# Projections beside the attention: steps of six products in place of twelve

## The chip, the cores and the metric

One core of a Trainium2 chip runs the whole kernel. The metric is the device time in microseconds (us), lower is better; the median of several runs stands for a kernel.

## The reference, cut to what matters

One layer of a decoder trunk on 1,024 tokens of width 1,024, with 16 learned meta tokens put ahead (1,040 positions). Everything is float32.

```python
h = h + 0.5 * swiglu(rms_norm(h, ffn1_norm), ffn1_w_in, ffn1_w_out)
u = rms_norm(h, mix_norm) @ w_in                 # 1024 -> 3584 columns
hq, hf, hi, hg, sq, sk, sv = split(u)            # 7 x 512 columns
o_hg = hgrn2(hq, hf, hi, hg, ...)                # gated linear recurrence, 4 heads of 128
o_sb = stick_breaking(sq, sk, sv, ...)           # causal attention, 8 heads of 64
h = h + concat(o_hg, o_sb) @ w_out
h = h + 0.5 * swiglu(rms_norm(h, ffn2_norm), ffn2_w_in, ffn2_w_out)
```

hgrn2 works in chunks of 128 positions; stick_breaking takes blocks of 128 queries: sigmoids of the scores, a running product of (1 - sigmoid) towards older keys, and the weighted sum of the values.

## The kernel before, in words

The kernel runs in stages, one after the other on TensorE (PE): the first feed-forward block; the projection `u`; attention; the recurrence; the output projection; the second feed-forward block. PE's order is written by hand (`manual_schedule`): PE executes in the order in which the Python code emits. The other engines are ordered by the framework.

**Products.** A matrix product of float32 quality is made of three products of rounded parts: each operand is split into a high and a low half (`wh`, `wl`; `xh`, `xl`), and for every k tile of 128 rows there are `wh*xh` (L249), `wl*xh` (L250) and `wh*xl` (L251). A projection column (128 columns of `w_in`) has 8 k tiles, so 24 products for each piece of positions. They add up in one PSUM bank.

**The projections of the recurrence** (`hgrn_fill`, L1118). There are 16 columns, in the order v, f, q, g for each of heads 0 to 3. A column of kind v or f is made in four pieces (264 or 256 positions), one of kind q or g in two halves of 512. The generator hands out a list of steps, each with a planned cost in ns; a step before is half of the k tiles of a piece, twelve products. After the last step of a piece, `use` (L1127) reads the bank out: a copy for v (L1135), two sigmoids for f (L1141, L1142), a sigmoid and then a VectorE product that reads the bank once more for q and g (L1149, L1150). The first step of a column issues the load of the next column's weights.

These steps are dealt out in three places.

1. *Projection stage* (`tasks`, L2153): the first two columns, through a planner called `weave`, beside preparation of the attention's operands, which has no PE instruction.
2. *The braid* (L1694): most of the other steps, beside the attention. Attention comes as 32 jobs (8 heads of 4 pairs of query blocks), one a round. A job's scores (tile `z`, L1640 and L1641) run in its own round, the transposes of its weights (`flip`, L1495 and L1549) two rounds later, the products with the values (`oacc`, L1570 and L1572) three rounds later. The transposes use two PSUM buffers, each freed when ScalarE (L1618) and VectorE (L1619) have split it into `wu` or `wm`. Scores go through two buffers, freed by two sigmoids (L1642, L1643), and then a scan on VectorE (L1646). All the projections of this stretch share one PSUM bank, since the other holds a constant (`begin`). In each round, projection steps are taken while a debt is positive, and are spread evenly over it:

```python
owed += share * sum(t for _, t, _ in now)   # share is 1.22
while owed > 0:
    step = next(fill, None)
    ...
    owed -= step[0]
now += [(at + (i + 0.5) / len(more), t, f) for i, (t, f) in enumerate(more)]
```

3. *The rest* (`rest`, L2201): what the braid has not taken and the last column (g of head 3), through `weave` (L1724) beside the recurrence heads 0, 1 and 2. The weave keeps a clock of planned PE time. A projection step adds its cost. A stage of a head adds its PE cost and then holds that head for a lag. The heads may start at 9000, 14000 and 19000. The choice here:

```python
ready = bool(live) and live[0][0] <= clock
if filling and join is None and (behind or not ready and (even or not live)):
    step = next(fill, None)
```

In this call `even` is always true and `behind` never, and the weave ends with the last projection step; stages that heads have not yet done are carried on by the next weave (L2267). That one mixes heads 0 to 3 with the 64 steps of three products of the first half of the output projection (tile `wo`, `mix_out`, 16 column tiles of four steps; weights in two buffers, attention's output in tiles `oT`), and there `behind` and `even` keep the steps spent in proportion to the heads' planned work.

**A recurrence head** (`hgrn_attend`, L1185) has these stages (planned PE cost, lag, in ns): loads (0, 4000); flips of v (960, 500); "own", 16 small matmuls (1740, 1700; L1235, then VectorE L1236 and L1239); seven levels for n = 1 to 64 (890, 1500 each; a copy on ScalarE L1264, eight matmuls L1270, two decays on VectorE L1257, and for n up to 16 a predicated copy on VectorE L1278, otherwise copies on ScalarE L1288); flips of k (960, 2000; L1299, L1306); states (1740, 2500; L1314, L1321, VectorE L1324); two outputs (1740, 3000; L1334, L1338); two closing flips (430, 0; L1354).

Of the kernel before, what the change touches and what calls it, by code (L numbers as in the profile page):

```python
# [22 lines left out]
KT = D // P  # L23
# [25 lines left out]
class Block:  # L49
# [1068 lines left out]
    def hgrn_fill(self, xh, xl, pool, dst):  # L1118

        nc = self.nc  # L1120
        plan, cols = self.heads_plan, self.columns_of_heads()
        self.stores, self.level_banks = [], "zo"

        def staged(n):
            return pool.tile([P, 512], F32, tag="st", name="st", bufs=4)[:, :n]

        def use(kind, h, ps, c0, n):  # L1127
            s = slice(c0, c0 + n) if kind in "vf" else slice(c0 - META, c0 - META + n)
            t = staged(n)
            if c0 >= HALVES[1][0] and kind != "g":  # L1130
                ps = ps[:, ::-1]
                at = s.start + HALVES[1][0] + T - 2 * c0 - n
                s = slice(at, at + n)
            if kind == "v":
                nc.scalar.copy(t, ps)  # L1135
                with self.tc.issue_after(self.last_load.ins):
                    nc.sync.dma_start(dst[kind][h, :, s], t)
                return
            elif kind == "f":
                k = staged(n)  # L1140
                nc.scalar.activation(t, ps, AF.Sigmoid)  # L1141
                nc.scalar.activation(k, ps, AF.Sigmoid, scale=-1.0)  # L1142
                nc.vector.tensor_scalar(
                    t, t, self.lbc[:, h : h + 1], self.lb[:, h : h + 1], ALU.mult, ALU.add
                )
                nc.vector.tensor_scalar_mul(k, k, self.lbc[:, h : h + 1])
                nc.sync.dma_start(dst["k"][h, :, s], k)
            else:
                nc.scalar.activation(t, ps, AF.Sigmoid)  # L1149
                nc.vector.tensor_mul(t, t, ps)  # L1150
            store = lambda: nc.sync.dma_start(dst[kind][h, :, s], t)
            if (kind, h) == plan[-1] and c0 == HALVES[1][0]:
                self.stores.append(store)
            else:
                store()

        kept = {}

        def part(i, ci, c0, n, half):
            if ci == 0 and half == 0:  # L1160
                kept["w"] = self.ahead_w.pop(cols[i])
                for c in cols[i + 1 : i + (3 if i == 0 else 2)]:
                    if c not in self.ahead_w:
                        self.ahead_w[c] = self.col_tile(self.a["w_in"][0], c)
                kept["round"] = self.rounds[cols[1]]
            if half == 0:
                kept["ps"] = self.proj_bank(n)
            self.product(
                kept["ps"], kept["w"], xh, xl, c0, n, range(4 * half, 4 * half + 4)
            )  # L1170
            if half == 1:
                with self.tc.issue_after(kept["round"]) if i == 0 else ExitStack():
                    use(*plan[i], kept["ps"], c0, n)

        for i, (kind, _) in enumerate(plan):
            for ci, (c0, n) in enumerate(PIECES if kind in "vf" else HALVES):
                for half in range(2):
                    yield 12 * (n * 0.42 + 13), lambda a=(i, ci, c0, n, half): part(*a)

    def level_bank(self, shape, name):  # L1180
        self.level_banks = self.level_banks[::-1]
# [592 lines left out]
    def run(self):  # L1774
        nc, tc, a = self.nc, self.tc, self.a
# [11 lines left out]
        n = 512  # L1787
# [8 lines left out]
        with ExitStack() as c0:  # L1796
            with ExitStack() as c1:
# [117 lines left out]
                with tc.manual_schedule(engines={nc.tensor.engine}), ExitStack() as c2:  # L1915
# [181 lines left out]
                    xh, xl = hat  # L2097
# [52 lines left out]
                columns = self.hgrn_fill(xh, xl, pst, hgD)  # L2150
                oH, self.att = [], []

                def tasks():  # L2153
                    done = []
                    for i in range(4):
                        for x in done[i - 2] if i > 1 else ():
                            yield "join", x
                        done.append(
                            (yield from self.sb_project(i, xh, xl, mixb, mix, (qD, kD, vD)))
                        )  # L2160
                        if i == 2:
                            next(jobs)
                    for t, f in islice(columns, 16):
                        f()
                        yield t

                with tc.manual_schedule(engines={nc.tensor.engine}):
                    cf = ExitStack()
                    fetch = self.pool("fetch", ctx=cf, side="right")
                    jobs = self.sb_jobs((qD, kD, vD, oD), fetch, self.att)  # L2170
                    with ExitStack() as c2:
                        mixb = self.pool("mixb", ctx=c2)
                        mix = self.pool("mix", ctx=c2)
                        self.weave(tasks())
                    with ExitStack() as c2:
                        self.att.append(self.pool("att1", ctx=c2))
                        tag = self.proj_tags[0]
                        self.proj_tags = [self.proj_tags[1]] * 2
                        self.begin = self.pproj.tile([P, 512], F32, tag=tag, name="begin", bufs=1)
                        nc.vector.memset(self.begin, 0.0)  # L2180
                        nc.vector.tensor_copy(self.begin[:, 1 : P + 1], self.ident[:, ::-1])
                        self.braid(jobs, islice(columns, 76), 1.22, 2.0, 3.0)
                    cf.close()
                    self.proj_tags[0] = tag
                    hg_ctx = ExitStack()
                    hg = self.pool("hg", ctx=hg_ctx, side="right")
                    heads = [self.hgrn_attend(h, hg, hgD, oH) for h in range(4)]
                    self.wide = hg.tile([P, 5, 512], U8, name="wide")
                    for i, n in enumerate(LEVELS[:5]):
                        m = self.masks[:, i, :].rearrange("p (b h r) -> p b h r", h=2, r=n)  # L2190
                        wide = self.wide[:, i].rearrange("p (h c x) -> p h c x", h=2, c=4)
                        for half in range(2):
                            for c in range(4):
                                nc.vector.tensor_copy(
                                    wide[:, half, c].rearrange("p (b r) -> p b r", r=n),
                                    m[:, :, 1 - half, :],
                                )
                    for h in range(3):
                        next(heads[h])

                    def rest():  # L2201
                        left = list(columns)
                        for t, f in left[:-1]:
                            f()
                            yield t
                        left[-1][1]()

                    self.weave(rest(), heads[:3], 1e6, 1.0, True)
# [183 lines left out]
```

## Time and profile before

| what | value |
|---|---|
| median of the runs | 1957.84 us (1956.85 to 1957.93, 3 runs) |
| profiled execution, its own time | 1959.65 us |
| span from first to last instruction | 1957.9 us |
| granted PE clock, mean | 0.999 |
| busy in the span: PE, VectorE (DVE), ScalarE (ACT), GpSimd (POOL) | 98%, 71%, 43%, 23% |

In the profile an instruction is named by its line in the kernel (L1270), its engine and the tiles it writes and reads (`out<-in`). PEld are the weight loads of PE. A row of a group gives count, busy us, mean ns of one instruction, the idle time of the engine before them and what ended it. A row of the waits says who waited for whom: us in total, times, longest. A matmul's shown length (0.39 us for 512 columns) overlaps the next; from start to start it is 0.23 us. SPq is the queue that issues most DMAs.

### The profile page before, as it was taken

The numbers are of one execution on the slowest core, as the hardware profiler recorded it, in microseconds if no ns is written. First come the engines' busy times: TensorE is split into PE (matmuls) and PEld (weight loads), VectorE is DVE, ScalarE is ACT, GpSimd is POOL, SyncE is SP. The second block draws the span as 40 slices with busy tenths as digits, with TensorE's granted clock in tenths as the row PEclk, the third lists the DMA queues.
The fourth block names the chain that finished last, engine by engine and source line by source line (L and its number), as shares of the span: only waits on it lengthen the run. The fifth ranks groups of instructions, "written<-read, shape, count | busy, mean of one in ns | idle before, by whom it ended". The sixth has DMA issues, their size and how long they took to land.

```text
span 1957.9 us, 30218 instructions
## 1 busy us (share of the span) xinstructions
PE 1919.8 (98%) x10607; PEld 1616.6 (83%) x10607; DVE 1390.4 (71%) x2184; ACT 849.6 (43%) x1711; POOL 450.5 (23%) x625
## 2 busy tenths in 40 slices
PE   7999999999999999999999999999999999999999
PEld 6888888788888888888898978887888888888887
DVE  7977877877678665467777766677567767766774
ACT  6523443334444544356666635433232332344443
POOL 3010100001000003133333332210544645530000
PEclk9999999999999999999999999999999999999999
DMA  7356887758965315865454177655634444469473
GB/s 213 93 165 170 253 272 243 233 203 291 375 221 188 127 54 144 193 170 148 128 148 121 57 253 225 161 208 183 198 115 140 128 131 121 132 243 318 154 231 113
DMA packets 381687, 355.54 MB, mean 182 GB/s; under 512 B 129040, under 2 KB 284560, under 8 KB 381536
## 3 DMA queue, kind: packets, MB, share of 16 engines
q1 hardware_dynamic: 359728, 288.98, 48.7%
q0 software_dynamic: 20768, 64.63, 9.5%
q8 instruction: 84, 1.38, 0.3%
q14 instruction: 67, 0.55, 0.1%
q10 hardware_dynamic: 1040, 0.00, 0.0%
HBM read 237.95 MB, written 115.57 MB: 181 GB/s over the span
## 4 chain that ended last, share of the span: by engine, by line
PE 89%; DVE 4%; DMA 3%; ACT 2%; issue 1%; POOL 1%; SPq 1%; DVEq 0%; ACTq 0%; POOLq 0%
PE o L732 21%; PE qb L450 18%; PE qa L450 12%; PE qc L450 12%; PE proj L249 5%; PE proj L251 4%; PE proj L250 4%; PE flip L1495 2%; PE wo L250 1%; PE wo L249 1%; PE wo L251 1%; PE mq L1001 1%; PE oacc L1572 1%; PE oacc L1570 1%; DMA oT<-oD 1%
## 5 line engine op out<-in xcount | busy, mean ns | idle before, releaser
L450 PE MATMUL qb<-T,wh 128*128 128x512 f32 x1056 | 344.6, 390 | 1.3 <-ACT T L309 0.8
L450 PEld LDWEIGHTS qb<-T,wh 128*128 128x128 f32 x1056 | 198.1, 188 | 46.4 <-issue 2.5
L450 PE MATMUL qa<-B,wh 128*128 128x512 f32 x696 | 226.7, 390 | 0.3 <-ACT B L835 0.2
L249 PE MATMUL proj<-xh,wh 128*128 128x512 f32 (+2 forms) x640 | 213.2, 333 | 2.6 <-ACT st L1142 1.3
L732 PE MATMUL o<-t,w 128*128 128x512 f32 x924 | 211.8, 390 | 0.7 <-DVE u L543 0.7
L251 PE MATMUL proj<-xl,wh 128*128 128x512 f32 (+2 forms) x640 | 210.2, 328 | 0.8 <-DVE xl L1957 0.8
L250 PE MATMUL proj<-xh,wl 128*128 128x512 f32 (+2 forms) x640 | 210.1, 328 | 0.0
L732 PE MATMUL o<-parts 128*128 128x512 f32 x924 | 209.6, 389 | 0.0
L450 PE MATMUL qb<-T,wl 128*128 128x512 f32 x528 | 205.5, 389 | 0.0
L732 PEld LDWEIGHTS o<-t,w 128*128 128x128 f32 x924 | 172.8, 188 | 37.8 <-ACT sgm L981 1.1
L732 PEld LDWEIGHTS o<-parts 128*128 128x128 f32 x924 | 173.5, 188 | 36.0
L362 DVE TENSOR_TENSOR wl<-s,wh 128x512 fp32r<-128x512 f32 x160 | 165.6, 1035 | 50.8 <-ACT wh L360 49.9
L360 ACT CAST wh<-s 128x512 fp32r<-128x512 f32 x160 | 99.2, 622 | 188.5 <-PE qb L450 141.1
L450 PEld LDWEIGHTS qa<-B,wh 128*128 128x128 f32 x696 | 130.5, 188 | 28.0 <-DVE B L836 0.5
L360 ACT CAST wh<-raw 128x512 fp32r<-128x512 f32 x120 | 74.4, 621 | 155.8 <-PE qc L450 111.4
L450 PE MATMUL qa<-B,wl 128*128 128x512 f32 x348 | 135.4, 389 | 0.0
L249 PEld LDWEIGHTS proj<-xh,wh 128*128 128x128 f32 x640 | 120.8, 189 | 15.0 <-ACT st L1142 2.2
L251 PEld LDWEIGHTS proj<-xl,wh 128*128 128x128 f32 x640 | 120.7, 189 | 12.3 <-DVE xl L1957 1.2
L250 PEld LDWEIGHTS proj<-xh,wl 128*128 128x128 f32 x640 | 120.8, 189 | 10.1
L450 PE MATMUL qc<-B,wh 128*128 128x512 f32 x352 | 115.1, 390 | 2.3 <-DVE u L543 2.3
L450 PE MATMUL qc<-T,wh 128*128 128x512 f32 x352 | 117.0, 394 | 0.0
L450 PEld LDWEIGHTS qb<-T,wl 128*128 128x128 f32 x528 | 99.1, 188 | 20.2
(393 smaller groups left out, 3819.4 us busy)
## 6 DMA issues: line engine op xcount, KB each, us to landing
raw<-in_ffn_w_in_dram SPq DMA_DIRECT2D x176, 256.0 KB, 4.0
raw<-in_ffn_w_out_dram SPq DMA_DIRECT2D x112, 256.0 KB, 4.5
w2in<-both SPq DMA_DIRECT2D x28, 512.0 KB, 3.4
raw<-in_w_in_dram SPq DMA_DIRECT2D x25, 512.0 KB, 5.2
ks<-kD SPq DMA_DIRECT2D x32, 260.0 KB, 4.8
wout<-both SPq DMA_DIRECT2D x16, 512.0 KB, 3.7
wh<-w2in SPq DMA_DIRECT2D x27, 256.0 KB, 3.1
wl<-w2in SPq DMA_DIRECT2D x27, 256.0 KB, 3.1
```

The lines of the kernel that those rows point to most:

```text
L249: nc.tensor.matmul(ps, wh[:, s], xs, start=k == 0, stop=False)
L250: nc.tensor.matmul(ps, wl[:, s], xs, start=False, stop=False)
L251: nc.tensor.matmul(ps, wh[:, s], xl[:, k, c0 : c0 + n], start=False, stop=k == nk - 1)
L360: nc.scalar.copy(hi, src)
L362: self.block_lo = nc.vector.tensor_sub(lo, src, hi.bitcast(F32))
L450: nc.tensor.matmul(ps, a[:, k, :], b[:, k, :], start=start and k == 0 and i == 0, stop=k == 3 and i == 2, skip_group_check=True,)
L732: nc.tensor.matmul(banks[bank][m], y[:, m * P : (m + 1) * P], z, start=start and at == 0 and e == 0, stop=q == nq - 1 and e == 2, skip_gro ...
L1001: nc.tensor.matmul(ps[at : at + 32, :], self.xm[:, 4 * h + k, :], got[i, h][:, k, :], start=h == 0 and k == 0, stop=h == 1 and k == 3, til ...
L1495: self.nc.tensor.transpose(ps[:m, j, :], src[:, s0 : s0 + m], self.ident)
L1570: nc.tensor.matmul(o[:, c], vj, w[0], start=j == 0, stop=False, skip_group_check=True)
L1572: nc.tensor.matmul(o[:64, c], vj[:, :64], w[1], start=False, stop=end, skip_group_check=True)
```

## The change

A step is now a quarter of a piece's k tiles, six products, with half the planned cost. The counts of steps that the projection stage and the braid may take are doubled, so that they name the same columns. Products, their order within a piece, loads, stores and readers are the same.

```diff
-        def part(i, ci, c0, n, half):
-            if ci == 0 and half == 0:
+        def part(i, ci, c0, n, at):
+            if ci == 0 and at == 0:
                 kept["w"] = self.ahead_w.pop(cols[i])
...
-            if half == 0:
+            if at == 0:
                 kept["ps"] = self.proj_bank(n)
-            self.product(
-                kept["ps"], kept["w"], xh, xl, c0, n, range(4 * half, 4 * half + 4)
-            )
-            if half == 1:
+            self.product(kept["ps"], kept["w"], xh, xl, c0, n, range(at, at + 2))
+            if at == 6:
                 with self.tc.issue_after(kept["round"]) if i == 0 else ExitStack():
                     use(*plan[i], kept["ps"], c0, n)
...
-                for half in range(2):
-                    yield 12 * (n * 0.42 + 13), lambda a=(i, ci, c0, n, half): part(*a)
+                for at in range(0, KT, 2):
+                    yield 6 * (n * 0.42 + 13), lambda a=(i, ci, c0, n, at): part(*a)
...
-                    for t, f in islice(columns, 16):
+                    for t, f in islice(columns, 32):
                         f()
                         yield t
...
-                        self.braid(jobs, islice(columns, 76), 1.22, 2.0, 3.0)
+                        self.braid(jobs, islice(columns, 152), 1.22, 2.0, 3.0)
```

## The prediction

> **What bounds the kernel now.** I read the page first: busy shares, then the chain of work that ended last.
>
> ```profile
> PE 1919.8 (98%) x10607; PEld 1616.6 (83%) x10607; DVE 1390.4 (71%) x2184; ACT 849.6 (43%) x1711; POOL 450.5 (23%) x625
> ...
> PE 89%; DVE 4%; DMA 3%; ACT 2%; issue 1%; POOL 1%; SPq 1%; DVEq 0%; ACTq 0%; POOLq 0%
> ```
>
> TensorE (PE) is the bound, and it takes its instructions in the written order. The change adds and drops no product, so it can only move PE's waits. Next, the stretches by stage: projections alone; attention with projections (the braid); the last projections; the recurrence heads with the output projection; then three windows around the one dip of the clock.
>
> ```profile
> 690.00:861.80 171.80, 169.39 (x1024) 149.83 (x1024) 96.41 (x159) 76.20 (x149) 36.36 (x59) 1.00 0.55 141
> 861.80:1135.35 273.55, 264.54 (x1837) 239.19 (x1835) 200.63 (x325) 178.83 (x460) 97.46 (x140) 0.99 0.43 122
> 1135.35:1146.46 11.11, 11.11 (x49) 8.91 (x49) 5.83 (x42) 2.23 (x4) 1.40 (x2) 1.00 0.80 285
> 1146.46:1156.80 10.34, 9.66 (x59) 8.21 (x58) 5.16 (x8) 3.59 (x6) 8.99 (x23) 1.00 1.03 393
> 1156.80:1274.00 117.20, 110.89 (x743) 95.93 (x742) 81.12 (x145) 58.11 (x158) 32.80 (x55) 1.00 0.72 201
> 864.10:867.50 3.40, 2.58 (x11) 1.68 (x12) 3.25 (x5) 3.13 (x9) 1.30 (x4) 0.96 0.86 228
> 867.50:870.95 3.45, 3.45 (x11) 2.72 (x10) 3.24 (x5) 1.24 (x5) 2.38 (x3) 0.54 1.03 214
> 1164.20:1167.60 3.40, 1.83 (x11) 1.08 (x10) 3.40 (x6) 0.67 (x1) 0.00 (x0) 1.00 1.00 350
> ```
>
> Columns: stretch, its length, then busy us of PE, PEld, DVE, ACT, POOL, granted clock, DMA share, GB/s. PE idles 9.0 us in the braid, 0.7 in the first heads' stages, 6.3 in the stage of the heads; nothing elsewhere is worth much. So the braid can give back at most 9.0 us, plus what the dip cost: 3.45 us at 0.54 is about 1.6 us. PE's waits in the braid:
>
> ```profile
> PE flip L1495 <- DVE wu L1619: 3.6, 9, 0.8
> PE z L1640 <- ACT sig L1643: 1.9, 5, 0.5
> PE flip L1495 <- DVE wm L1619: 1.8, 3, 0.6
> PE proj L249 <- DVE st L1150: 0.9, 2, 0.7
> ```
>
> **Part 1: the braid's order.** Its rule is arithmetic on planned costs, so I followed it round by round for both costs (2736 or 1368 ns for a 512-wide step). Both deal the same work: 74 steps before, 148 after, because in both the debt of 1.22 times the attention's planned time is paid off with 5472 ns of work unspent. Before, a block of twelve products stands between groups of attention steps; after, blocks of six, twice as often. The flips wait for the split of the flip two before (VectorE, wu and wm, 5.4 us together); with six products between most of them that wait goes almost wholly: minus 5.0. The score products wait for the sigmoids of the two tiles before (1.9 us), nearly all in the first rounds, where round 1 gets a step it had not: minus 0.5. The dip of the clock follows these first rounds (PE busy 2.58 of 3.40 us in the window ahead of it): it may go or move, minus 0.8 (0 to 1.6).
>
> Against it: in the braid all projections share one PSUM bank. The first product of a piece waits until the piece before has been read out.
>
> ```profile
> 1078.76 0.39 PE L251 MATMUL proj<-xl,wh 128*128 128x512 f32 x1
> ...
> 1079.19 0.60 ACT L1149 ACTIVATE st<-proj 128x512 f32<-128x512 f32 x1 [1.24 <-PE proj L251]
> 1079.82 0.69 DVE L1150 TENSOR_TENSOR st<-st,proj 128x512 f32<-128x512 f32 x1 [1.15 <-ACT st L1149]
> ...
> 1080.56 0.39 PE L249 MATMUL proj<-xh,wh 128*128 128x264 f32 x1 [0.66 <-DVE st L1150]
> ```
>
> ```profile
> L1141 ACT ACTIVATE st<-proj 128x264 f32<-128x264 f32 (+1 forms) x12 | 4.7, 388 | 8.3 <-PE proj L251 8.3
> ...
> L1135 ACT COPY st<-proj 128x264 f32<-128x264 f32 (+1 forms) x12 | 4.5, 378 | 6.6 <-PE proj L251 6.6
> ```
>
> The last product of a q or g piece ends at 1079.15; its two readers release the bank 1.4 us later (1080.56). For f, two overlapped reads of 0.39 make about 0.75; for v, one copy of 0.38 makes about 0.47. What covers this is the attention work on PE between two steps. At each of the 37 piece borders I added it up (a score pair 0.3 to 0.5 us, a 128-wide flip 0.11, a value pair 0.23). Before, only 3 borders fall short, 0.9 us in all, which is the 0.9 the waits show. After, the cover is halved: the first q piece has 0.91 us of attention behind it where it had 1.81, and 22 borders fall short by 7.4 us in all. Plus 6.5. The sum of part 1 is about 0 (bounds: minus 10.5, all waits and the dip gone and no border waiting; plus 8, the borders wait and nothing goes).
>
> **Part 2: the last projections.** After the braid, 6 steps are left before, 12 after, the same work. They are dealt by the weave beside heads 0 to 2, whose first stage may start once the planner's clock reaches 9000. Before, the clock steps by 2736: the fourth step makes 10944, head 0's flips go in, and two steps are left. One goes ahead of "own" of head 0 and the flips of head 1, then the last step ends this weave. The timeline has just that:
>
> ```profile
> 1146.46 1.30 PE L1495 MATMUL flip<-ident,vT 128*16 128x128 f32 x9
> 1147.51 0.48 PE L249 MATMUL proj<-xh,wh 128*128 128x512 f32 x1
> ...
> 1150.37 1.95 PE L1235 MATMUL lvl<-QA,KB 128*128 128x128 f32 x16
> 1152.15 0.71 PE L1495 MATMUL flip<-ident,vT 128*16 128x128 f32 x5
> ...
> 1156.82 1.07 PE L1270 MATMUL lvl<-QA,KP 128*128 128x128 f32 x8
> 1157.73 1.95 PE L1235 MATMUL lvl<-QA,KB 128*128 128x128 f32 x16
> ```
>
> After, the clock steps by 1368: the seventh step makes 9577, with five steps left. Head 0's flips, step 8, own of head 0, step 9 (clock 15013), head 1's flips, level 1 of head 0, own of head 1, level 2 of head 0, head 2's flips follow. Here is the catch: this weave takes a projection step only when no head is ready. A level adds 890 to the clock and holds its head for 1500; with three heads going, another head is always ready. So step 10 comes only when all three are held, which my sum reaches after 18 of the 21 levels (heads 0 to 2 have seven each); steps 11 and 12 follow with the last levels, the state sums and the first output of head 0 between. Only then does the next weave bring the output projection. So nearly all of three heads' level work, which had output products between it, now runs on PE with four half-size steps beside it. VectorE's share:
>
> ```profile
> L1278 DVE COPY_PREDICATED attn<-wide,lvl 128x512 f32<-128x512 uint8 x20 | 18.8, 941 | 0.0
> ...
> L1257 DVE TENSOR_TENSOR KB<-KB,Ts 128x512 f32<-128x512 f32 x24 | 16.9, 716 | 1.6 <-ACT KP L1264 1.6
> L1257 DVE TENSOR_TENSOR QA<-QA,Ts 128x512 f32<-128x512 f32 x24 | 16.4, 684 | 2.7 <-PE lvl L1270 2.7
> ...
> L1324 DVE SCALAR_TENSOR_TENSOR F<-F,Ts,up 128x128 f32<-128x128 f32 x28 | 9.7, 346 | 3.5 <-PE up L1321 2.6
> ...
> L1239 DVE TENSOR_TENSOR attn<-lvl,ident 128x512 f32<-128x512 f32 x8 | 5.5, 689 | 4.4 <-PE lvl L1235 4.4
> ...
> L1236 DVE TENSOR_TENSOR QA<-QA,F 128x1024 f32<-128x1024 f32 x4 | 5.1, 1280 | 0.4 <-PE lvl L1235 0.2 <-DMA wh<-wout 0.2
> ```
>
> From the end of head 0's own to the last projection step: 15 levels up to 16 at 0.716 + 0.684 + 0.941 = 2.34 (35.1), 6 larger levels at 1.40 (8.4), three owns at 1.28 + 2 x 0.689 = 2.66 (8.0), head 0's states 8 x 0.346 (2.8): 54.3 us of VectorE, of which the last level's 1.4 may lag. With some 2 us of idle until three heads run, 5% of handovers (2.6), and the last level and step on PE (0.9 + 1.4) the stretch takes about 60 us. PE's work in it: 21 levels at 0.91 (1157.73 less 1156.82), two owns at 1.78, two flips at 1.05, four steps at 1.43 (half of 1150.37 less 1147.51), 50 small matmuls of states, keys and outputs at 0.11: 36 us. PE idles about 23 us there (bounds 15, VectorE running a level of each head behind the end; 30, handovers three times as dear). PE cannot fill it: the output products come later in its order.
>
> **Part 3: the stage behind.** The 64 output steps keep their rate against the heads' work left, so about half stay over as one block at the end. The waits of the old stage:
>
> ```profile
> PE knp L1306 <- DVE kms L1300: 1.6, 3, 0.7
> PE wo L251 <- DMA oT<-oD: 1.5, 1, 1.5
> PE flip L1495 <- ACT vr L1223: 1.4, 2, 0.7
> ...
> PE wo L250 <- DMA wl<-wout: 0.8, 1, 0.8
> ```
>
> Half of its some 7 us of waits goes, with fewer changes between kinds of matmul (minus 5). The oT loads, which can start only when the last projection has freed its memory, meet the first output steps a little sooner (plus 1). Head 3 runs its levels nearly alone (plus 1.5). In the closing block each column tile takes four steps, 2.8 us, and its weights have two buffers:
>
> ```profile
> DMA to landing us min/median/max: 2.5/4.3/8.5
> ```
>
> At 2.5 us the load hides, at 4.3 each tile takes (2.8 + 4.3) / 2 = 3.55: 0 to 6 us over eight tiles; I take 3. SP's queue: the two loads of g that move ahead of the oT loads wait for key flips that PE passes before its last projection step, so they hold up nothing; all other DMAs keep their order. The 32 steps in the projections' own stage stand beside work without PE instructions: 0.
>
> **Sum.** 0 + 23 - 5 + 1 + 1.5 + 3 = about +23 us (bounds of the pieces together: +9 to +36). The profiled execution took 1959.65 us with a span of 1957.9; the median of the runs is 1957.84, so I add to that: 1980.
>
> **Rivals.**
> *Half clock in the heads' stretch.* PE would be busy 36 of 60 us, in pieces under a microsecond. For: the window with 2.58 of 3.40 busy was followed by one at 0.54. Against: the window at 1164.2 had 1.83 of 3.40 and no dip. At half clock throughout, PE's 36 us become 72, over VectorE's 60: plus 12; in alternate windows about plus 5. Time 1985 to 1992. The Trainium skill, "TensorE: Matmul & The Clock Gate", section "A second HAM failure mode: psum-queue depth-cycling", says that frequent micro-idles between groups of matmuls make the clock swing between half and full rate. By that rule this rival would be the outcome; of the two windows, one agrees and one does not.
>
> *Faster: the braid decides.* If VectorE is not the limit of the heads' stretch, since its operations overlap the level matmuls of other heads well enough to stay within PE's 36 us plus the waits that go, only part 1 and the 5 us of part 3 are left. With the dip gone and the borders costing half: minus 4 to minus 9, 1949 to 1954. It decides once the stretch idles under some 5 us; that needs VectorE's 54 us to shrink by a third, and the rows say no.
>
> *No change.* The same, with the borders at their full 6.5 us: the parts cancel, 1956 to 1960.
>
> **How the numbers follow.** Main case 0.65 (1972 to 1988, with part 2's 15 to 30), half clock 0.20, smaller (plus 4 to 14) 0.07, faster 0.04, no change 0.04. A measurement of this kernel can tell about 0.2%, 4 us, from no change. Range 1966 to 1994. Faster 0.04, same 0.04, slower 0.92.
>
> **What would show it.** Right: after the braid a stretch of some 60 us with PE near 60% and VectorE over 90% busy, with no output product in it, and a block of some 33 output steps ahead of the second half of that projection; PE proj waiting for st (L1149, L1150, L1142) by 5 us or more in the braid, flip waits under 1.5. Wrong: output products or projection steps between most levels; VectorE under 80% in that stretch, which would make the handovers and not its work the limit; or braid waits that grow beyond 9 us.

## The result

The change makes the kernel slower: 2001.52 us (median of 6 runs, 1998.84 to 2004.27) against 1957.88 us; ratio 1.0221, 95% interval 1.0208 to 1.0235. The sign and the larger cause, the heads drawn ahead of the last projections, were forecast. The loss in the braid was not, and the size was not: 43.6 us more, forecast about 22, and the time lies above the range. The profiled execution took 1998.84 us, with a span of 1996.9 us, 39.0 more than before. It was the fastest of the six, and the profiled one of before was slower than its median, so the profiles show less than the medians.

The page of the changed kernel, busy shares and the group of the first product of each triple (count, busy us, mean ns, then the idle time of PE before them); below them the same group before:

```profile
PE 1931.3 (97%) x10607; PEld 1622.5 (81%) x10607; DVE 1395.9 (70%) x2184; ACT 854.0 (43%) x1713; POOL 455.5 (23%) x625
...
L249 PE MATMUL proj<-xh,wh 128*128 128x512 f32 (+2 forms) x640 | 216.7, 339 | 13.0 <-DVE st L1150 7.7
...
L249 PE MATMUL proj<-xh,wh 128*128 128x512 f32 (+2 forms) x640 | 213.2, 333 | 2.6 <-ACT st L1142 1.3
```

As many matmuls as before; their idle time before the first product is 13.0 us where it was 2.6. The stretches by stage, with the columns of the prediction (braid; last projections up to head 0's own; from there to the last projection; heads with output steps; closing block):

```profile
861.80:1142.66 280.86, 266.28 (x1843) 239.04 (x1841) 205.78 (x326) 181.54 (x459) 98.56 (x140) 1.00 0.43 121
1142.66:1156.75 14.09, 14.09 (x74) 11.70 (x74) 6.95 (x45) 3.60 (x6) 2.62 (x4) 1.00 0.82 285
1156.75:1210.52 53.77, 42.10 (x294) 37.86 (x293) 48.97 (x78) 23.60 (x54) 20.29 (x47) 0.94 0.21 78
1210.52:1276.00 65.48, 58.93 (x387) 51.13 (x385) 36.15 (x73) 33.38 (x101) 18.80 (x20) 0.97 0.75 219
1276.00:1313.10 37.10, 27.09 (x102) 19.25 (x100) 2.61 (x4) 5.72 (x10) 6.87 (x8) 0.95 0.97 275
```

PE idles 14.6 us in the braid (9.0 before) and 28.2 us in the last three (7.0 in the two stretches that they replace). The granted clock, 1.00 there before, falls to 0.94 to 0.97. The waits of PE over all of these stretches (who, for whom, us, times, longest; lines behind the change stand two earlier than before):

```profile
PE proj L249 <- DVE st L1150: 7.7, 11, 1.5
PE lvl L1268 <- ACT KP L1262: 7.2, 7, 1.8
PE wo L249 <- DMA wh<-wout: 6.4, 5, 2.4
PE wo L250 <- DMA wl<-wout: 4.0, 6, 1.1
PE flip L1493 <- ACT vr L1221: 3.4, 1, 3.4
PE proj L249 <- ACT st L1142: 2.6, 7, 0.7
PE op L1332 <- DVE vT L1346: 1.8, 1, 1.8
...
PE flip L1493 <- DVE wu L1617: 1.3, 4, 0.4
PE z L1638 <- ACT sig L1641: 1.0, 2, 0.6
```

The first, sixth and two last rows are the braid: the flips' waits fell from 5.6 us to 2.2 (0.9 of it in a row for L1547 that is not shown), the borders' rose from 0.9 to 11.1 (0.8 of it at the copies of v, L1135). The others are the stages behind it. That the order is the one worked out shows in head 0's own and in the first and last output step, in the changed kernel and, in the last row, before:

```profile
1155.04 1.95 PE L1233 MATMUL lvl<-QA,KB 128*128 128x128 f32 x16
...
L249 PE MATMUL wo<-oT,wh x64: 387/397/775, 1220.6 to 1312.4; 128*128 128x512 f32 x64
...
L249 PE MATMUL wo<-oT,wh x64: 389/476/504, 1163.2 to 1272.5; 128*128 128x512 f32 x64
```

They run from 1220.6 on, 66 us after head 0's own began, with only four projection steps of six products among the heads' work in between. Before, they began at 1163.2, 13 us after it.

### The profile page after: what moved, and what is told of

It reads as the page before. It is cut to its first block, busy times and chain, and to the rows that moved or that the text cites. A ratio compares the mean times of both kernels' runs of the same rounds, so it can differ in the third digit from the quotient of the medians.

```text
span 1996.9 us, 30233 instructions
## 1 busy us (share of the span) xinstructions
PE 1931.3 (97%) x10607; PEld 1622.5 (81%) x10607; DVE 1395.9 (70%) x2184; ACT 854.0 (43%) x1713; POOL 455.5 (23%) x625
## 4 chain that ended last, share of the span: by engine, by line
PE 87%; DVE 4%; DMA 3%; ACT 3%; issue 1%; POOL 1%; SPq 0%; DVEq 0%; ACTq 0%; POOLq 0%
PE o L732 21%; PE qb L450 17%; PE qa L450 12%; PE qc L450 12%; PE proj L249 4%; PE proj L251 4%; PE proj L250 4%; PE flip L1493 1%; PE wo L250 1%; PE wo L251 1%; DMA wl<-wout 1%; PE wo L249 1%; PE mq L1001 1%; PE oacc L1568 1%; PE oacc L1570 1%
## 5 line engine op out<-in xcount | busy, mean ns | idle before, releaser
L249 PE MATMUL proj<-xh,wh 128*128 128x512 f32 (+2 forms) x640 | 216.7, 339 | 13.0 <-DVE st L1150 7.7
L249 PEld LDWEIGHTS proj<-xh,wh 128*128 128x128 f32 x640 | 120.4, 188 | 31.0 <-DVE st L1150 10.8
```

The lines of the kernel that those rows point to most:

```text
L249: nc.tensor.matmul(ps, wh[:, s], xs, start=k == 0, stop=False)
```

## The experiments

In the first five, steps of six can be rejoined to steps of twelve at each place by itself:

```python
def paired(steps):
    for t, f in steps:
        u, g = next(steps)
        yield t + u, lambda f=f, g=g: (f(), g())
```

These six lines more move the kernel down: L255 in these runs is L249, L1156 is L1150.

**1. The fine steps in the braid alone.** Projection stage and rest take joined steps:

```diff
-                    for t, f in islice(columns, 32):
+                    for t, f in islice(paired(columns), 16):
...
-                        left = list(columns)
+                        left = list(paired(columns))
```

> Steps of six products in the braid alone; the projection stage and the last projections beside heads 0 to 2 keep steps of twelve, so that the heads' order is that of before. Theory (two separate costs: the shared PSUM bank in the braid, and the heads drawn ahead of the last projections): about 1964 us, 6 above before, with waits of PE proj for st of about 11 us in the braid and a heads' stage as before. Rival (the step size itself costs, by more changes between kinds of matmul, wherever it is used): 1975 or more. Rival of the prediction (the braid comes out even): 1958.

1967.77 us, ratio 1.0051 (1.0035 to 1.0068): plus 9.7, where 6 was expected. PE's waits in the braid:

```profile
PE proj L255 <- DVE st L1156: 7.7, 11, 1.5
PE proj L255 <- ACT st L1148: 3.9, 8, 1.3
PE z L1644 <- ACT sig L1647: 1.7, 2, 1.0
PE flip L1553 <- DVE wu L1623: 1.6, 2, 1.2
PE flip L1499 <- DVE wu L1623: 1.3, 4, 0.4
PE proj L255 <- ACT st L1141: 0.8, 3, 0.4
```

The borders are there as in the changed kernel (1.3 of the second row stands ahead of the braid, before too). The braid does not come out even, and the heads' stage is as before. The profiled execution (span 1964.5 us, 6.6 more than before) shows less than the median: it was the fastest of this run's four. In it the waits grew by 6.8: borders plus 10.2, flips and scores minus 3.4 (4.6 us where it was 8.0). The dip of the clock that went takes some 1.6 off, so about 1.4 us stay open. Whether more changes between kinds of matmul cost that is not shown; the 1975 of that rival is ruled out.

**2. The fine steps in the rest alone.**

```diff
-                        self.braid(jobs, islice(columns, 152), 1.22, 2.0, 3.0)
+                        self.braid(jobs, islice(paired(columns), 76), 1.22, 2.0, 3.0)
```

(and the projection stage as in 1).

> Steps of six products only for the last projections beside heads 0 to 2; projection stage and braid as before. Theory: the whole loss from the heads' order, some 32 to 36 us, so 1990 to 1994, with a stretch of some 54 us without output products, VectorE about 90% busy in it, and weight waits of some 10 us in the closing block of output steps. Rival (the order of the heads is harmless and the braid's delay spoils what follows): below 1965.

1988.95 us, ratio 1.0157 (1.0142 to 1.0172): plus 30.9, just under the 1990 expected. From head 0's own to the last projection, the stage with output steps, and the closing block:

```profile
1149.50:1202.40 52.90, 41.15 (x293) 36.46 (x293) 48.16 (x78) 23.55 (x54) 23.40 (x46) 0.97 0.22 78
1202.40:1268.00 65.60, 59.60 (x399) 52.16 (x398) 39.27 (x76) 35.06 (x104) 19.52 (x21) 1.00 0.75 228
1268.00:1305.00 37.00, 27.70 (x89) 19.87 (x88) 0.10 (x1) 4.11 (x7) 6.02 (x8) 0.82 0.92 263
```

VectorE is busy 48.2 of 52.9 us. Runs 1 and 2 together make 40.6 of the 43.6 us. The two parts are nearly separate; the remaining 3 us lie within the intervals of these measurements.

**3 and 4. Two banks in the braid**, with the fine order (3) and with that of before (4). The constant `begin` goes to a spare place in SBUF, the tile `edge`:

```diff
-        self.pool("edge", side="right").tile([P, 504], F32, name="edge")
+        self.edge = self.pool("edge", side="right").tile([P, 504], F32, name="edge")
...
-                        tag = self.proj_tags[0]
-                        self.proj_tags = [self.proj_tags[1]] * 2
-                        self.begin = self.pproj.tile([P, 512], F32, tag=tag, name="begin", bufs=1)
+                        self.begin = self.edge
...
-                    self.proj_tags[0] = tag
```

> As the first run (steps of six in the braid alone), and the constant that occupies the second PSUM bank of the projections lies in SBUF instead, so that the projections alternate between two banks. Theory (border waits come from the shared bank, and the finer order does remove the flips' waits): the 11 us of waits for st go, 1952 to 1955, below before. Rival (the attention's chain through ScalarE and VectorE limits the braid, and the bank's waits are only where it shows): the waits come back at flips and scores, 1961 to 1964.

> The order of before with the two banks of the run above. Theory: before had 0.9 us of waits at borders, so 1956 to 1958. If reading the constant from SBUF made the scan slower or faster, this run would show it by itself: above 1960 or below 1955.

Run 3: 1958.70 us (1.0004, 0.9995 to 1.0013), between the theory and its rival. Run 4: 1961.88 us (1.0020, 1.0011 to 1.0030). With two banks the waits for st in the braid are gone, and the fine order gains 9.1 us over run 1. But the waits of flips and scores went from 4.6 to 12.0 us, as the rival had it, and the time did not come below before. Run 4 shows why: the constant's place costs by itself, 3.8 us in the order of before. The scan in runs 1 and 3:

```profile
L1650 DVE TENSOR_TENSOR_SCAN keep<-keep,begin 128x144 f32<-128x144 f32 (+6 forms) x112 | 97.9, 876 | 20.6 <-ACT keep L1646 15.0 <-POOL keep L1639 3.0 <-POOL sig L1657 0.8
```

```profile
L1650 DVE TENSOR_TENSOR_SCAN keep<-keep,edge 128x144 f32<-128x144 f32 (+6 forms) x112 | 127.2, 1139 | 11.8 <-ACT keep L1646 8.3 <-POOL keep L1639 2.0
```

With the constant in SBUF a scan takes 1139 ns on average, not 876. VectorE is held 29 us longer by its scans, and the flips wait longer for it. Not every scan is slower, though. The same shape, begun while GpSimd runs its product on `sig`, in runs 1 and 3:

```profile
1027.39 1.57 POOL L1657 TENSOR_TENSOR sig<-sig,keep 128x784 f32<-128x784 f32 x1 [5.35 <-ACT sig L1647]
1027.92 0.43 DVE L1650 TENSOR_TENSOR_SCAN keep<-keep,begin 128x144 f32<-128x144 f32 x1
...
1023.24 1.58 POOL L1657 TENSOR_TENSOR sig<-sig,keep 128x784 f32<-128x784 f32 x1 [4.37 <-DVE keep L1650]
1023.76 1.37 DVE L1650 TENSOR_TENSOR_SCAN keep<-keep,edge 128x144 f32<-128x144 f32 x1
```

In run 3 the scan ends 0.3 us behind the product, in run 1 half a microsecond ahead of it. Of run 3's 112 scans 44 begin while GpSimd is at work, and 42 of these carry all of the 29 us; the other 70 take what they take in run 1. With that handicap on both sides, the fine order is 3.2 us faster than the coarse one by the medians. That this is the gain of the flips which the prediction had set against the borders is not shown: the waits of flips and scores are alike in the profiles of runs 3 and 4 (12.0 and 11.7 us). The largest of each:

```profile
PE flip L1499 <- DVE wu L1623: 8.9, 10, 1.6
...
PE flip L1499 <- DVE wu L1623: 8.0, 14, 1.2
```

**5. Early release of the one bank.** As run 1, but q and g pieces are copied out first:

```diff
-                nc.scalar.activation(t, ps, AF.Sigmoid)
-                nc.vector.tensor_mul(t, t, ps)
+                k = staged(n)
+                nc.scalar.copy(k, ps)
+                nc.scalar.activation(t, k, AF.Sigmoid)
+                nc.vector.tensor_mul(t, t, k)
```

> As the first run (steps of six in the braid alone, one bank), but a q or g piece is first copied out of the bank by ScalarE, and sigmoid and product read the copy: the bank is free after one read of 0.6 us, not after 1.4 us. Theory (the braid's loss is the bank's readout): the 7.7 us of waits for the product on VectorE shrink to 1 or less, the 4.7 us at f and v borders stay; 1960 to 1963. Rival (the attention's chain is the limit and takes the place of these waits): 1966 or more.

1963.69 us (1.0029, 1.0019 to 1.0039), 4.1 less than run 1:

```profile
PE flip L1501 <- DVE wu L1625: 4.5, 7, 1.7
PE proj L255 <- ACT st L1148: 3.9, 8, 1.3
PE flip L1555 <- DVE wu L1625: 1.6, 2, 1.2
```

The 7.7 us for the VectorE product are gone altogether, and 4 us come back at the flips (2.9 us in run 1; 6.9 here, with 0.8 for `wm` that is not shown). So both are partly right: the bank's readout by VectorE holds PE up, and the chain through VectorE is next in line and takes half of it back. Net, the early release is worth 4.1 of the 9.7 us.

**6. Less work for VectorE in the heads' stretch.** The changed kernel, with this in `level`, where `in_rest` holds while the rest runs. It leaves out 15 copies that the layer needs, so its result is not the layer's:

```diff
+            if n <= 16 and self.in_rest:
+                return
             if n <= 16:
                 nc.vector.copy_predicated(
```

> The changed kernel, with the predicated copies (VectorE, 0.94 us each) of the levels up to 16 left out while the last projections run, 15 of them, 14 us of VectorE. Theory (the heads' stretch is bound by VectorE): it shortens by 10 to 14 us, total 1988 to 1991. Rival (latency from engine to engine or the halved clock bounds it): by less than 4 us, 1998 or more.

1987.87 us, 13.7 less than the changed kernel. The same stretch:

```profile
1156.75:1201.00 44.25, 39.17 (x294) 34.91 (x293) 37.18 (x63) 23.65 (x54) 20.33 (x42) 1.00 0.25 88
```

VectorE's busy time fell by 11.8 us and the stretch by 9.5, up to 3 of which is the clock, 1.00 where it was 0.94. VectorE bounds the stretch; the rival's limit was 4 us.

**7. More work for PE there.** Each level's matmuls twice, again while the rest runs:

```diff
-            for c in range(4):
+            for c in [c for c in range(4) for _ in range(1 + self.in_rest)]:
                 nc.tensor.matmul(
                     ps[:, :, c, :],
```

> The changed kernel, with each level's matmuls issued twice into the same bank while the last projections run: 21 levels times 0.9 us, 19 us more work for PE in that stretch, with the same result. Theory (PE idles there behind VectorE): most of it goes into the idle time and dips of the clock in the stretch go, so plus 0 to 6 us, 2001 to 2008. Rival (PE or its clock is the limit): plus 15 or more, 2016.

2003.31 us, plus 1.8:

```profile
1155.84:1213.80 57.96, 55.99 (x463) 53.17 (x462) 48.89 (x78) 24.79 (x55) 18.51 (x44) 1.00 0.21 75
```

168 more matmuls, 13.9 us more of PE's busy time, lengthened the stretch by 4.2 us and the kernel by 1.8. PE's idle time there was real: 11.7 us, now 2.0. The dips of the clock in the stretch (0.94) are gone (1.00); in the stages behind it this profile has more of them than the changed kernel's (20 us at half clock, not 7).

**8. Four buffers for the output weights**, in the changed kernel, and as a control (**9**) in the kernel before:

```diff
-                    self.weights("wo", 2, 2, c1)
+                    self.weights("wo", 2, 4, c1)
```

> The changed kernel, with four buffers in place of two for the weights of the output projection. Theory (about a third of the heads' loss is the closing block of output steps, which outruns the loads of its weights): the 10.4 us of waits for wh and wl shrink under 2, and the dip of the clock in that block goes: 1989 to 1994. Rival (the loads are short of bandwidth, not of buffers): waits stay above 7, 1998 or more.

> The kernel before, with four buffers in place of two for the weights of the output projection. Theory: before has 0.9 us of waits for these weights, so 1956 to 1958, at most 1 us better; the 12 us that the buffers gave the changed kernel belong to its closing block.

Run 8: 1989.16 us, 12.4 less than the changed kernel. Its waits for these weights:

```profile
PE wo L250 <- DMA wl<-wout: 2.3, 3, 1.3
...
PE wo L249 <- DMA wh<-wout: 0.6, 1, 0.6
```

They went from 10.4 to 2.9 us, and there is no dip of the clock behind 1216 us. So the loads were short of buffers more than of bandwidth. Run 9: 1956.64 us (0.9990, 0.9981 to 0.9999), 1.9 us less than before where at most 1 was expected; that is 0.1%, about as small as this kernel's measurement can tell. The block is what needs the buffers.

**10. All last projections ahead of the heads**, in steps of six:

```diff
-                    self.weave(rest(), heads[:3], 1e6, 1.0, True)
+                    drain(rest())
```

> The changed kernel with steps of six everywhere, but the last twelve steps are all run ahead of the heads; the heads' stages all go to the weave with the output projection. Theory (the step size does no harm there by itself; the loss is the stages of the heads that stand alone, without output steps beside them): as the run with the fine braid alone, 1966 to 1971, no weight waits in a closing block and no dip of the clock. Rival (small steps in the last projections cost by themselves): above 1980.

1975.42 us (1.0086, 1.0072 to 1.0099): 26 less than the changed kernel, but 7.6 more than run 1, above what was expected. PE's waits behind the braid, three of the largest:

```profile
PE flip L1493 <- DVE vm L1218: 2.4, 1, 2.4
...
PE wo L249 <- DMA oT<-oD: 1.8, 1, 1.8
PE flip L1493 <- DMA vT<-hg_v: 1.3, 1, 1.3
```

The loss goes with the stages of the heads that stand alone. Of the step size itself the run says nothing: with no stage between them, twelve steps of six are the same instructions as six of twelve. Some head work beside the last projections seems worth having: without it PE waits for loads of the heads (`vT`) and of the output steps (`oT`), and the clock, expected without a dip, is at 0.83 from 1160 to 1180 us. Which of these makes the 7.6 us is not shown.

## Why the prediction was wrong

The order was right in every step: flips of head 0 after the seventh step, own after the eighth, the tenth step after 18 levels. VectorE bounds the stretch behind it, as forecast. What failed is the sum. Its step "the braid comes out even" was wrong (0, measured plus 9.7), the closing block was put at 3 us of waits (9.6), and PE's time lost to half clock was left to a rival (7 us). The idle time of the stretch was put too high (23, measured 11.7), which hid part of the rest.

*Part 1, the braid: forecast 0, measured plus 9.7 (run 1).* The number of borders that wait was nearly right, 21 where 22 were forecast. The flips and scores gave back 3.4 us in run 1 and 4.8 in the changed kernel (forecast 5.5), and the dip of the clock there went. The borders cost 11.1 us of waits (7.7 + 2.6 + 0.8), not 7.4. Part of this is the 1.4 us for the release of a q or g piece. In the kernel before, VectorE begins its product 0.03 us behind ScalarE at all 13 of these borders in the braid. In the changed kernel it does so at nine; at four it comes 0.2 to 1.0 us late. The longest:

```profile
883.13 2.10 DVE L234 TENSOR_TENSOR wl<-raw,wh 128x1024 fp32r<-128x1024 f32 x1 [0.42 <-ACT wh L232]
...
883.98 0.60 ACT L1149 ACTIVATE st<-proj 128x512 f32<-128x512 f32 x1 [0.52 <-PE proj L251]
...
884.59 0.28 PE L1570 MATMUL oacc<-wu,v 128*64 128x256 f32 x1
...
885.15 0.54 DVE L1617 TENSOR_TENSOR wu<-flip,wu 128x384 fp32r<-128x384 f32 x1
885.62 0.67 DVE L1150 TENSOR_TENSOR st<-st,proj 128x512 f32<-128x512 f32 x1
...
886.35 0.50 PE L249 MATMUL proj<-xh,wh 128*128 128x512 f32 x1 [1.48 <-DVE st L1150]
```

ScalarE is done at 884.58, VectorE starts its product 1.04 us later, and the bank is held 2.4 us. VectorE was busy with the split of the next weights (L234, 2.10 us) and of `wu`, which stand ahead of the product in its order. In the new order the product no longer always meets a free VectorE; the release of the old order was taken for the new one. The longer holds make 2.6 us in all, of the 3.7 that the borders exceed their forecast by. The other 1.1 us stay open.

*Part 2, the stretch: forecast some 60 us with PE idle 23; measured 53.8 us with 11.7 idle.* VectorE is 91% busy in it, and runs 6 and 7 confirm that it is the bound. The term was too large for two reasons. The lengths of VectorE's operations add up to 55.1 us, near the 54.3 of the sum, but VectorE is busy for 49.0: an operation begins before the one ahead of it has ended (in the fence above, the product 0.07 us before the split of `wu` ends), and the sum added lengths that overlap. And PE's own work takes longer than the 36 us of the sum: 39.2 at full clock (run 6), 42.1 here, partly at half clock.

*Part 3, the closing block: forecast plus 3, measured 9.6 us of waits for weights, 10.4 with the stage ahead of it.* With the dip that goes along, run 8 puts it at 12.4 us. The number of tiles, eight, was right. The landing time of a load was not: the formula was fed with 2.5 to 4.3 us, the lowest and the median of the old stage, and even 4.3 gives only 6 us. In the block, with the DMA share at 0.97, the medians are some 40% longer (KB each, median us to landing):

```profile
wh<-wout SPq DMA_DIRECT2D x12, 256.0 KB, 5.9
wl<-wout SPq DMA_DIRECT2D x12, 256.0 KB, 6.5
```

*The half clock* was a rival with 0.20. It came beside the main case, not in its place. The lost clock in the last three stretches is 0.06 x 53.8 + 0.03 x 65.5 + 0.05 x 37.1 = 7 us. The idle time there is 21.2 us more (28.2 less 7.0). That this is close to the 23.5 us which the terms of parts 2 and 3 add up to is luck: the stretch was put 11 too high, the closing block 7 too low. Together the two make 28 of the 31.8 us by which this part of the profile grew; about 3.5 stay open. The six executions had a granted clock of 0.992 to 0.997 over the whole span (0.999 to 1.000 in the kernel before). The profiled one had the highest, so by this measure half clock took more than these 7 us in the others. The Trainium skill, "TensorE: Matmul & The Clock Gate", section "A second HAM failure mode: psum-queue depth-cycling", says that frequent micro-idles between groups of matmuls make the clock swing between half and full rate. The trace agrees for three of the four dips, which came behind several waits of 0.4 to 1.8 us in a row; the first came behind a single wait of 3.4 us. The two dips of the stretch were gone when run 7 filled its waits.

The 32 steps of the projection stage cost nothing that these runs can tell: PE is busy 169.4 of its 171.8 us before and after.

## What to carry to other kernels

A finer grain changes what a planner's thresholds let through: follow its rule to the end of the list, past the place that is being tuned, and look for a step that is taken only when nothing else is ready. Work that leaves its cover costs twice, once where it stands alone and once in the block that it leaves behind, where buffers sized for an interleaved stage no longer hide their loads. A bank shared by successive pieces needs cover for its readout in the queues of the new order, not for the readout that the old one showed. And lengths read from a profile overlap: a sum of them is more than the time that the engine is busy.

## What the runs showed of the hardware

The scan on VectorE with its second operand in PSUM took 876 ns on average over its shapes, and 1139 ns with the same constant in SBUF (runs 1 and 3; 1144 in run 4). The whole difference lies in scans that began while GpSimd was at work: in run 3 these ended 0.3 to 1.0 us behind GpSimd's instruction (1.37 us for the shape that took 0.43 beside the same instruction with its operand in PSUM). Alone, the scan was as fast from either place.

The granted clock fell in windows of 3.4 us, not for the whole of a thinly used stretch: the changed kernel's stretch had 0.94 with PE busy 42.1 of 53.8 us, and run 6 had 1.00 with 39.2 of 44.3. The first of four windows at half clock, with the window ahead of it, and two windows without a dip:

```profile
1165.25:1168.66 3.41, 1.22 (x11) 1.22 (x12) 3.41 (x6) 1.63 (x3) 3.25 (x7) 1.00 0.05 16
1168.67:1172.08 3.41, 3.41 (x18) 3.41 (x18) 3.41 (x6) 1.35 (x3) 3.41 (x10) 0.50 0.03 7
...
1195.97:1199.38 3.41, 1.62 (x12) 1.47 (x12) 3.41 (x7) 2.39 (x7) 3.25 (x4) 1.00 0.43 159
1199.38:1202.79 3.41, 3.41 (x25) 2.84 (x24) 2.77 (x7) 0.49 (x1) 0.64 (x2) 1.00 0.00 0
```

PE was busy 1.2 to 1.4 us of the window ahead of each of the four; the window with 1.6 us in the third row was not followed by a dip. The dip in the kernel before, behind 2.58 of 3.40 us, does not fit this and stays unexplained.
